# TensorE in source order for the whole kernel, and modulation matmuls released in other groups

## The chip, the cores and the metric

The kernel runs on one core of one Trainium2 chip. The metric is the device time of one execution in microseconds (us). TensorE multiplies matrices, VectorE and ScalarE do elementwise work, SyncE issues the DMA transfers. In the rows below PE is TensorE's matmuls, PEld its weight loads, DVE VectorE, ACT ScalarE, and SPq SyncE's queue.

## The reference, cut to what matters

Two layers run on 384 tokens: 128 context tokens and 256 denoising tokens, with 2048 channels in 16 blocks of 128. For one layer:

```
shift, scale, gate = split(silu(c) @ w_mod + b_mod)            # per channel, for two condition vectors
h = rmsnorm(x) * (1 + scale) + shift
f_x,f_g, p_x,p_g, q,k,v,a_g, c_a,c_b,c_g = split(h @ w_in)     # 11 chunks of 512
y = concat(fourier(f_x) w_f * silu(f_g),  pool(p_x) w_p * silu(p_g),
           rmsnorm(diff_attention(q,k,v)) * silu(a_g),  conv_module(c_a,c_b) * silu(c_g)) @ w_out
x = x + gate * y
```

After the second layer the result is normalized and written token by token. The arithmetic is in 32 bits. A large product is made of three matmuls: each operand is split into a rounded part (hi) and a rest (lo), and hi·hi, hi·lo and lo·hi are summed in one PSUM bank.

## The kernel before, in words

**Main matmuls.** The input chunks are computed one after the other by `in_chunk` (L447): eight weight tiles of two 128-blocks each, loaded into a raw buffer (`rawp`, five of them), split by ScalarE (`hi`, L219) and VectorE (`lo`, L220) into buffers that hold three tiles (`hip` and `lop`, six halves each), and used by 24 matmuls (`main_tile`, L439, `mm3`, L434) into four PSUM banks (`mm`). The output projection (L920 to L942) does the same in four groups of 512 channels, g = 0 to 3. In the last group one 128-block is completed after the other. `finish_block` (L901) adds a finished block to x, and in the second layer scales it by final_g on ScalarE and transposes it on TensorE into `otp` (L918), in the order of the source right behind the group's last main matmul.

**Tasks.** Smaller branches are Python generators in a list `tasks`: `attention` (L585), `fourier`, `small_proj`, `pool_proj`, `conv_norm`. After every tile of 24 main matmuls `pump` (L347) is called. It calls `step` (L376), which advances each task to its next `yield`. A task's step takes a small PSUM tile with `sm` (L103; three buffers) for its matmuls. The number of yields between two parts of a task is the number of main tiles that the source puts between them. `finish` (L371) advances a task to its end at once, with no main tile between its parts. It is called in `gate` (L858): the chunk A_G is computed, then `finish(at)` ends the attention, then the gate is multiplied, and the next chunk, F_G, follows. At that point of the source the attention still has to normalize its last head, transpose it (`asT`), multiply it by the values (`aso`), normalize the heads (`otok`) and transpose twelve blocks (`oT`).

**Modulation.** shift, scale and gate of what is still to come are computed by two queues of items in `pump`: `fill["pe"]`, items of one 512 KB load (`mraw`) and small 32-column matmuls into `mod` (`mod_item`, L253, matmuls at L277), and `fill["dve"]`, items computed on VectorE (`side_item`, sums on TensorE as `mds`). At each pump `rate` is added to `due`; the `pe` queue is released when two items are due (`BP`). In layer 0 there are 48 such items at 48/78 per pump, in layer 1 twelve at 12/45. Four more are issued at the layers' border (`pe_mods`).

**Who sets the order.** The kernel is written for a planner that takes the instructions in source order as priorities and orders each engine's queue by estimated times: an instruction whose operands it expects late is passed by later ones. `manual_schedule(engines=...)` takes the named engines out of the planning and keeps them in source order. Before, it holds SyncE and TensorE until `in_order.close()` (L825), that is, through the first four chunks of layer 0; after that the planner orders both. ScalarE and VectorE are planned throughout. Weight loads and their splitting run at a raised priority (`ahead`, L206) after L825.

Of the kernel before, what the change touches and what calls it, by code (L numbers as in the profile page):

```python
# [55 lines left out]
def mixer_step(  # L56
# [11 lines left out]
    NB1, NB2 = 2, 2  # L68
    YA = 5
    BP = 2  # L70
    WARM = 24

    one = ctx.enter_context(tc.tile_pool(name="one", bufs=1))
# [19 lines left out]
    def nm(s):  # L93
        uid[0] += 1
        return f"{s}_{uid[0]}"
# [4 lines left out]
    def cvtile(s):  # L100
        return cvp.tile([P, 4, 432], F32, tag="cv", name=nm(s))

    def sm(s, shape=(P, 512)):  # L103
        return smp.tile(list(shape), F32, tag="sm", name=nm(s))

    def tt(out, a, b, op, eng=None):
# [32 lines left out]


    in_order = ExitStack()
    in_order.enter_context(tc.manual_schedule(engines={mybir.EngineType.SP, mybir.EngineType.PE}))

    o1 = CONST_OFF["ident"][0] + P
    nc.sync.dma_start(out=cst[:, :o1], in_=consts[:, :o1])
# [13 lines left out]
    xd = [drp.tile([P, 4, NT], F32, tag=f"xd{g}", name=f"xd{g}") for g in range(4)]  # L159

    idle = sm("idle")
    for _ in range(WARM):
        nc.tensor.matmul(idle, lhsT=ones, rhs=cmod.rearrange("p k c -> p (k c)"), start=True, stop=True)  # L163
# [149 lines left out]
    def side_item(l, kind, b0, k0):  # L313
        pool = side_pool[0]
        key = (l, kind, b0)
        if k0 == 0:
            side_acc[key] = gtile(pool, "macc", (P, 2, 512))
        acc = side_acc[key]
        raw = gtile(pool, "sraw", (P, 2, 512))
        c0 = MOD.index(kind) * D + b0 * P  # L320
        with ahead():
            nc.sync.dma_start(out=raw, in_=w_src("w_mod", l, k0, c0))
        for j in range(2):
            for v in range(2):
                cv = cmod[:, k0 + j, v:v + 1]
                if k0 + j == 0:
                    nc.vector.tensor_scalar(out=acc[:, v, :], in0=raw[:, j, :], scalar1=cv, scalar2=None, op0=ALU.mult)
                else:
                    stt(acc[:, v, :], raw[:, j, :], cv, acc[:, v, :], ALU.mult, ALU.add)
        if k0 + 2 == KC:  # L330
            del side_acc[key]
            ps = sm("mds", (P, 2, 4, 32))
            av = acc.rearrange("p v (b n) -> p v b n", n=P)
            for v in range(2):
                for q in range(4):
                    qs = slice(32 * q, 32 * q + 32)
                    nc.tensor.matmul(ps[qs, v], lhsT=ones[:, 0:32], rhs=av[:, v, :, qs])
            T = one.tile([P, 2, 4, 32], F32, tag="S", name=nm("T"))
            nc.vector.transpose(out=T.rearrange("p v b n -> p (v b n)"), in_=ps.rearrange("p v b n -> p (v b n)"))
            mod_store(l, kind, b0, 4, T[:, :, :, 0].rearrange("p v b -> p b v"))  # L340

    fill = {"pe": [], "dve": []}
    rate = {"pe": 0.0, "dve": 0.0}
    due = {"pe": 0.0, "dve": 0.0}
    burst = {"pe": BP, "dve": 1}

    def pump(flush=False):  # L347
        step()
        for e, item in (("pe", mod_item), ("dve", side_item)):
            due[e] += rate[e]  # L350
            if fill[e] and (due[e] >= burst[e] or flush):
                n = len(fill[e]) if flush else int(due[e])
                for _ in range(min(n, len(fill[e]))):
                    due[e] -= 1.0
                    item(*fill[e].pop(0))
            if not fill[e]:
                due[e] = 0.0
# [7 lines left out]
    def advance(gen):  # L365
        try:
            next(gen)
        except StopIteration:
            tasks.remove(gen)
# [4 lines left out]
                advance(gen)  # L374

    def step():  # L376
        for gen in list(tasks):
            advance(gen)

    def share(l, units, n_side):  # L380
        n_pe = len(units) - n_side
        for i in range(n_pe):
            kind, b0 = units[i]
            if i % 2 == 0 and i + 1 < n_pe and units[i + 1] == (kind, b0 + 4):
                fill["pe"].extend(mod_wide(l, kind, b0))
            elif not (i % 2 and units[i - 1] == (kind, b0 - 4)):
                fill["pe"].extend(mod_items(l, ((kind, b0, 4),), 2))
        for kind, b0 in units[n_pe:]:
            fill["dve"].extend(side_items(l, kind, b0))
# [18 lines left out]
    def bcast_tokens(r):  # L408
        dg = tmpp.tile([P, TB, P], F32, tag="t1", name=nm("dg"))
        for t in range(TB):  # L410
            nc.vector.tensor_scalar(out=dg[:, t, :], in0=ident, scalar1=r[:, t:t + 1], scalar2=None, op0=ALU.mult)
        bc = sm("bc")
        nc.tensor.matmul(bc[:, :NT], lhsT=ones, rhs=dg.rearrange("p t k -> p (t k)"))
        return bc
# [32 lines left out]
    def in_chunk(l, ci, hh, hl):  # L447
        ps4 = [mmp.tile([P, 512], F32, tag="mm", name=nm("mm")) for _ in range(4)]
        for kt in range(8):
            hi, lo = wtile(w_src("w_in", l, 2 * kt, ci * BR))  # L450
            main_tile(ps4, hi, lo, (2 * kt, 2 * kt + 1), hh, hl, kt == 0, kt == 7)
            pump()
        return ps4

    def v_chunk(l, hh, hl):
        ps3 = [mmp.tile([P, 512], F32, tag="mm", name=nm("mm")) for _ in range(TB)]
        for kt in range(8):
            hi, lo = wtile(w_src("w_in", l, 2 * kt, V_ * BR))
            for j in range(2):
                kc = 2 * kt + j  # L460
                g, kb = divmod(kc, 4)
                for t in range(TB):
                    ts = slice(t * P, (t + 1) * P)
                    st = kt == 0 and j == 0
                    sp = kt == 7 and j == 1
                    nc.tensor.matmul(ps3[t], lhsT=hh[g][:, kb, ts], rhs=hi(j), start=st, stop=False)  # L466
                    nc.tensor.matmul(ps3[t], lhsT=hh[g][:, kb, ts], rhs=lo(j), start=False, stop=False)  # L467
                    nc.tensor.matmul(ps3[t], lhsT=hl[g][:, kb, ts], rhs=hi(j), start=False, stop=sp)  # L468
            pump()
        return ps3  # L470
# [308 lines left out]
    for l in range(DEPTH):  # L779
# [141 lines left out]
        for g in range(4):  # L921
            ps4 = [mmp.tile([P, 512], F32, tag="mm", name=nm("mm")) for _ in range(4)]
            if g < 3:
                for i, kt in enumerate(order):
                    hi, lo = wtile(w_src("w_out", l, 2 * kt, g * BR))
                    main_tile(ps4, hi, lo, (2 * kt, 2 * kt + 1), yh, yl, i == 0, i == 7)
                    pump()
# [34 lines left out]
    n = 0  # L962
# [130 lines left out]
```

## Time and profile before

| What | Value |
|---|---|
| median of three runs | 1260.34 us (1260.25 to 1261.93) |
| the profiled execution | 1259.32 us, span 1257.5 us |
| mean granted TensorE clock | 0.993 |
| busy share: PE, PEld, DVE, ACT | 98%, 91%, 73%, 44% |
| chain that ended last | PE 86%, DVE 7%, DMA 3% |

The span runs from the first to the last instruction. A matmul's duration in the trace overlaps with that of the next one, so the pitch (start to start) is what a matmul costs when many follow each other. A plain 32-bit matmul has two records (the 24 of the warm-up are 48), a main matmul or a transpose has one.

### The profile page before, as it was taken

What the parts mean: (1) busy time and instruction counts of PE and PEld (TensorE: products, weight loads), DVE (VectorE), ACT (ScalarE), POOL (GpSimd) and SP (SyncE); (2) the same over time, 40 slices, a digit from 0 to 9 for tenths busy, and PEclk for the clock granted to TensorE, in tenths of its full rate; (3) what the DMA queues carried; (4) which work ended last, traced back from release to release, by engine and by line L of the source; (5) the groups of instructions that cost most, each with busy time, mean ns of one, the idle gap of its engine ahead of it and who ended that gap; (6) DMA issues with size and microseconds to landing.
All of it is one profiled execution on the core that took longest, in us unless ns stands there. A gap on an engine that the chain in (4) does not pass through costs nothing.

```text
span 1257.5 us, 22096 instructions
## 1 busy us (share of the span) xinstructions
PE 1229.7 (98%) x8558; PEld 1145.4 (91%) x8558; DVE 921.6 (73%) x1788; ACT 555.8 (44%) x1116; POOL 2.1 (0%) x34
## 2 busy tenths in 40 slices
PE   8899999999999999999999999999999999999995
PEld 4899998798998999999998999979999999999995
DVE  3588788999965965998977559998455795647452
ACT  4533233344547545432235533334554765344442
POOL 0000000000000000000000000000000000000000
PEclk9899999999999999999999999999999999999998
DMA  6898887543446865888955444444223563645322
GB/s 239 294 354 313 299 307 274 176 170 116 149 157 206 287 232 188 312 307 306 333 204 184 160 151 159 159 160 149 94 88 115 176 243 118 201 156 187 118 67 101
DMA packets 70712, 251.85 MB, mean 200 GB/s; under 512 B 7760, under 2 KB 8912, under 8 KB 70608
## 3 DMA queue, kind: packets, MB, share of 16 engines
q1 hardware_dynamic: 70608, 250.45, 56.6%
q8 instruction: 67, 1.10, 0.3%
q14 instruction: 37, 0.30, 0.1%
HBM read 243.08 MB, written 7.34 MB: 199 GB/s over the span
## 4 chain that ended last, share of the span: by engine, by line
PE 86%; DVE 7%; DMA 3%; issue 2%; ACT 1%; SPq 0%; DVEq 0%; ACTq 0%
PE mm L435 23%; PE mm L437 22%; PE mm L436 22%; PE mod L277 4%; DVE cacc L110 2%; DVE lo L107 2%; PE idle L163 2%; PE mm L466 2%; PE mm L467 2%; PE mm L468 2%; DMA mraw<-in_w_mod_dram 1%; DMA sraw<-in_w_mod_dram 1%; PE sp L435 1%; PE sp L436 1%; PE sp L437 1%
## 5 line engine op out<-in xcount | busy, mean ns | idle before, releaser
L116 ACT ACTIVATE hi<-raw 128x512 fp32r<-128x512 f32 x498 | 309.1, 631 | 537.1 <-PE mm L436 349.0
L107 DVE TENSOR_TENSOR lo<-raw,hi 128x512 fp32r<-128x512 f32 x498 | 336.4, 687 | 213.5 <-ACT hi L116 204.6
L435 PE MATMUL mm<-hh,hi 128*128 128x384 f32 x1280 | 440.3, 345 | 5.3 <-ACT hh L113 5.2
L436 PE MATMUL mm<-hl,hi 128*128 128x384 f32 x1280 | 432.4, 338 | 0.0
L437 PE MATMUL mm<-hh,lo 128*128 128x384 f32 x1280 | 432.1, 338 | 0.0
L435 PEld LDWEIGHTS mm<-hh,hi 128*128 128x128 f32 x1280 | 241.5, 189 | 24.0 <-issue 9.9
L436 PEld LDWEIGHTS mm<-hl,hi 128*128 128x128 f32 x1280 | 241.8, 189 | 0.9 <-DVE hl L110 0.2
L437 PEld LDWEIGHTS mm<-hh,lo 128*128 128x128 f32 x1280 | 241.6, 189 | 0.3 <-DVE lo L107 0.3
L435 PE MATMUL mm<-yh,hi 128*128 128x384 f32 x512 | 173.5, 340 | 1.7 <-DVE xr L110 1.7
L436 PE MATMUL mm<-yl,hi 128*128 128x384 f32 x512 | 172.4, 337 | 0.0
L437 PE MATMUL mm<-yh,lo 128*128 128x384 f32 x512 | 172.4, 337 | 0.0
L110 DVE SCALAR_TENSOR_TENSOR macc<-sraw,cmod,macc 128x512 f32<-128x512 f32 x210 | 147.3, 743 | 8.1 <-DMA sraw<-in_w_mod_dram 8.1
L110 DVE SCALAR_TENSOR_TENSOR cacc<-u,cst,cacc 128x399 f32<-128x399 f32 x232 | 146.5, 631 | 6.0 <-ACT cacc L113 1.6
L435 PEld LDWEIGHTS mm<-yh,hi 128*128 128x128 f32 x512 | 96.2, 188 | 5.5 <-issue 3.6
L436 PEld LDWEIGHTS mm<-yl,hi 128*128 128x128 f32 x512 | 96.3, 188 | 0.0
L437 PEld LDWEIGHTS mm<-yh,lo 128*128 128x128 f32 x512 | 96.2, 188 | 0.0
L107 DVE TENSOR_TENSOR acc<-acc,mm 128x384 f32<-128x384 f32 x128 | 65.8, 551 | 25.9 <-PE mm L437 25.8
L277 PE MATMUL mod<-mraw,cmod 128*32 128x128 f32 (+2 forms) x1920 | 73.9, 290 | 1.4 <-DMA mraw<-in_w_mod_dram 0.9
L277 PEld LDWEIGHTS mod<-mraw,cmod 128*32 128x32 f32 x1920 | 48.0, 109 | 21.7 <-issue 11.5
L113 ACT ACTIVATE hh<-ht,AB 128x128 fp32r<-128x128 f32 x64 | 27.3, 451 | 26.4 <-DVE ht L110 25.6
L466 PE MATMUL mm<-hi,hh 128*128 128x512 f32 x96 | 38.3, 399 | 0.0
L467 PE MATMUL mm<-lo,hh 128*128 128x512 f32 x96 | 38.0, 396 | 0.0
(209 smaller groups left out, 956.7 us busy)
## 6 DMA issues: line engine op xcount, KB each, us to landing
raw<-in_w_in_dram SPq DMA_DIRECT2D x172, 512.0 KB, 4.4
mraw<-in_w_mod_dram SPq DMA_DIRECT2D x136, 512.0 KB, 4.6
raw<-in_w_out_dram SPq DMA_DIRECT2D x64, 512.0 KB, 4.3
sraw<-in_w_mod_dram SPq DMA_DIRECT2D x56, 512.0 KB, 5.7
xT<-in_x_dram SPq DMA_DIRECT2D x4, 768.0 KB, 6.7
xr<-in_x_dram SPq DMA_DIRECT2D x4, 768.0 KB, 7.0
xd<-xr SPq DMA_DIRECT2D x4, 768.0 KB, 5.8
xr<-xd SPq DMA_DIRECT2D x4, 768.0 KB, 5.9
```

The costliest lines, as they stand in the source:

```text
L107: (eng or nc.vector).tensor_tensor(out=out, in0=a, in1=b, op=op)
L110: nc.vector.scalar_tensor_tensor(out=out, in0=a, scalar=s, in1=b, op0=op0, op1=op1)
L113: nc.scalar.activation(out=out, in_=a, func=func, **kw)
L116: nc.scalar.activation(out=out, in_=a, func=AF.Copy, scale=scale)
L163: nc.tensor.matmul(idle, lhsT=ones, rhs=cmod.rearrange("p k c -> p (k c)"), start=True, stop=True)
L277: nc.tensor.matmul(ps[qs, 0:nb * 32].rearrange("p (b n) -> p b n", n=32), lhsT=cmod[:, k0 + j, :], rhs=raw[:, j, :, qs], start=(k0 + j == ...
L435: nc.tensor.matmul(ps, lhsT=wh, rhs=ah, start=start, stop=False)
L436: nc.tensor.matmul(ps, lhsT=wh, rhs=al, start=False, stop=False)
L437: nc.tensor.matmul(ps, lhsT=wl, rhs=ah, start=False, stop=stop)
L466: nc.tensor.matmul(ps3[t], lhsT=hh[g][:, kb, ts], rhs=hi(j), start=st, stop=False)
L467: nc.tensor.matmul(ps3[t], lhsT=hh[g][:, kb, ts], rhs=lo(j), start=False, stop=False)
L468: nc.tensor.matmul(ps3[t], lhsT=hl[g][:, kb, ts], rhs=hi(j), start=False, stop=sp)
```

## The change

TensorE's source order is entered on the kernel's own context, so it lasts to the end; SyncE's ends where it did. `pump` learns from `step` whether a task took a small PSUM tile in this step (`visits`), and releases the items of the `pe` queue when two are due and there was such a visit, or when four are due (`LATE`). Nothing that is computed changes.

```diff
+    LATE = 4
...
+    visits = []
+
     def sm(s, shape=(P, 512)):
+        visits.append(s)
         return smp.tile(list(shape), F32, tag="sm", name=nm(s))
...
     in_order = ExitStack()
-    in_order.enter_context(tc.manual_schedule(engines={mybir.EngineType.SP, mybir.EngineType.PE}))
+    ctx.enter_context(tc.manual_schedule(engines={mybir.EngineType.PE}))
+    in_order.enter_context(tc.manual_schedule(engines={mybir.EngineType.SP}))
...
     def pump(flush=False):
-        step()
+        visit = step()
         for e, item in (("pe", mod_item), ("dve", side_item)):
             due[e] += rate[e]
-            if fill[e] and (due[e] >= burst[e] or flush):
+            ready = due[e] >= (burst[e] if visit or e == "dve" else LATE)
+            if fill[e] and (ready or flush):
                 n = len(fill[e]) if flush else int(due[e])
...
     def step():
+        n = len(visits)
         for gen in list(tasks):
             advance(gen)
+        return len(visits) > n
```

## Rows read from the trace of the kernel before

**Rows 1.** The page's first part: busy us, share, instructions.

```profile
PE 1229.7 (98%) x8558; PEld 1145.4 (91%) x8558; DVE 921.6 (73%) x1788; ACT 555.8 (44%) x1116; POOL 2.1 (0%) x34
```

**Rows 2.** Window of tile mm alone in layer 1: us, PE, PEld, DVE, ACT, clock, DMA.

```profile
715.00:740.00 25.00, 25.00 (x146) 25.00 (x145) 0.00 (x0) 0.00 (x0) 1.00 0.38 128
```

**Rows 3.** Timeline of PE, first phase: start, us, instruction, idle before it.

```profile
64.85 0.64 PE L277 MATMUL mod<-mraw,cmod 128*32 128x128 f32 x16 [0.61 <-DMA mraw<-in_w_mod_dram]
```

**Rows 4.** Timeline of PE around a run of two modulation items.

```profile
255.91 0.34 PE L437 MATMUL mm<-hh,lo 128*128 128x384 f32 x1
256.18 1.07 PE L277 MATMUL mod<-mraw,cmod 128*32 128x256 f32 x16
257.18 0.45 PE L435 MATMUL mm<-hh,hi 128*128 128x384 f32 x1
257.46 0.34 PE L436 MATMUL mm<-hl,hi 128*128 128x384 f32 x1
```

**Rows 5.** Timeline of PE around a run of four items.

```profile
94.98 1.96 PE L277 MATMUL mod<-mraw,cmod 128*32 128x128 f32 x64
96.86 0.44 PE L435 MATMUL mm<-hh,hi 128*128 128x384 f32 x1
```

**Rows 6.** Timeline of PE, two items behind an attention step.

```profile
351.83 1.07 PE L277 MATMUL mod<-mraw,cmod 128*32 128x256 f32 x16
352.83 0.44 PE L435 MATMUL mm<-hh,hi 128*128 128x384 f32 x1
```

**Rows 7.** DMA issues, the page's sixth part: count, KB each, us to landing.

```profile
mraw<-in_w_mod_dram SPq DMA_DIRECT2D x136, 512.0 KB, 4.6
```

**Rows 8.** Timeline of PE at the end of layer 0's attention.

```profile
384.37 0.60 PE L640 MATMUL scs<-acc,acc 64*128 64x256 f32 x4
...
392.07 0.52 PE L657 MATMUL asT<-cst,pt 128*128 128x128 f32 x3
...
403.07 0.51 PE L680 MATMUL oT<-cst,otok 128*128 128x128 f32 x3
```

**Rows 9.** Windows of tile mm alone, where the planner moved TensorE's work.

```profile
384.97:403.30 18.33, 15.76 (x75) 12.98 (x75) 0.00 (x0) 1.25 (x3) 1.00 0.77 261
976.95:995.35 18.40, 16.41 (x81) 14.03 (x82) 0.00 (x0) 1.24 (x3) 1.00 0.54 184
1136.13:1141.80 5.67, 5.26 (x25) 4.07 (x25) 2.08 (x6) 0.00 (x0) 1.00 0.56 187
```

**Rows 10.** Timeline of ACT beside the first of these windows.

```profile
388.97 0.62 ACT L116 ACTIVATE hi<-raw 128x512 fp32r<-128x512 f32 x1
...
399.54 0.64 ACT L116 ACTIVATE hi<-raw 128x512 fp32r<-128x512 f32 x1
```

**Rows 11.** Timeline of PE in layer 1's output projection, behind group 0.

```profile
1138.23 0.49 PE L918 MATMUL otp<-cst,xr 128*128 128x128 f32 x3
...
1141.51 0.55 PE L918 MATMUL otp<-cst,xr 128*128 128x128 f32 x3
```

**Rows 12.** Timeline of DVE, then of PE, behind group 3's first block.

```profile
1216.60 0.74 DVE L110 SCALAR_TENSOR_TENSOR xr<-mm,GT,xr 128x128 f32<-128x128 f32 x2 [0.84 <-PE mm L437]
...
1218.65 0.50 PE L918 MATMUL otp<-cst,xr 128*128 128x128 f32 x3
```

**Rows 13.** Windows of all instructions (POOL before the clock), and a timeline row of PE.

```profile
36.00:43.00 7.00, 6.45 (x20) 6.21 (x21) 2.22 (x4) 3.93 (x9) 0.00 (x0) 0.51 0.63 253
670.00:675.00 5.00, 3.19 (x37) 1.62 (x36) 3.61 (x14) 2.78 (x7) 0.00 (x0) 1.00 0.91 311
...
36.55 0.69 PE L435 MATMUL mm<-hh,hi 128*128 128x384 f32 x1 [3.27 <-ACT hh L113]
```

**Rows 14.** Timeline of PE at the layers' border.

```profile
669.66 0.83 PE L418 MATMUL st<-ones,xsq 128*128 128x1 f32 x6
...
672.27 0.91 PE L413 MATMUL bc<-dg,ones 128*128 128x384 f32 x2
```

**Rows 15.** Timeline of PE inside a Fourier step of layer 0.

```profile
292.05 1.05 PE L277 MATMUL mod<-mraw,cmod 128*32 128x256 f32 x10
```

## The prediction

> **What bounds the kernel now.** I read the page's busy shares first: TensorE is busy for 1229.7 us of a span of 1257.5, VectorE for 921.6, ScalarE for 555.8 [rows 1]. So what TensorE doesn't do, or does at half clock, is added to the time. Next I took TensorE's timeline and cut it into islands: stretches of anything but main matmuls between two main matmuls. A main matmul alone has a pitch of 25.00 us over some 144.3 (146 touch the window, two are cut by its edges), 0.173 us [rows 2]. Then I laid the timeline beside the source. Nearly every island stands where the source has it. The reader is to see the exceptions [rows 8, 9, 11]: there the planner let main matmuls of the next chunk pass an instruction whose operands were late. The timelines of ScalarE and VectorE show why they were late [rows 10, 12].
>
> **Part 1: other groups of modulation matmuls.** In a run of two items the first record is 0.27 us behind the last main matmul, the run takes 1.00, and the next main pitch is 0.28 instead of 0.173 [rows 4]. A run of four takes 96.86 - 94.98 = 1.88 [rows 5]. So an item is (1.88 - 1.00) / 2 = 0.44, and a run by itself has a fixed cost of 0.12 in it, 0.10 on entering and 0.11 on leaving: 0.32. Two items behind an attention step take 352.83 - 351.83 = 1.00 again [rows 6], and there entering and leaving, 0.20, are paid by that step.
> By the source, the 48 items of layer 0 at 0.615 per pump are now 24 runs of two, 16 of them alone, and layer 1's twelve are six runs, five alone. With the visits and LATE I count 15 runs in layer 0 (7 alone) and 4 in layer 1 (2 alone). Eleven runs fewer at 0.12, and twelve fewer alone at 0.20: 1.3 + 2.4 = 3.7 us gained. Bounds: nothing (the cost goes with the item), and 5. The loads come in fours on SyncE's queue, 512 KB and 4.6 us each [rows 7], and hold four of the five raw buffers. Two converted weight tiles, 2 x 24 x 0.173 = 8.3 us of matmuls, and the fifth buffer cover that, so I add nothing; without that cover one run would wait about one landing, 4.6 us.
>
> **Part 2: source order to the end.** It costs wherever TensorE's next instruction has late operands. SyncE's and GpSimd's queues aren't reordered by the edit after the first phase. What stands behind a late instruction on TensorE is the next chunk's main matmuls, and on those wait the evacuations, the freeing of hi and lo, and so the weight loads. That source order does block is seen in the first phase, where TensorE waits 0.61 us for a modulation load with main matmuls behind it [rows 3].
>
> *End of the attention, once per layer.* Behind the last tile of A_G, `finish(at)` issues asT, aso and oT with nothing between them. In layer 0 they end 18.33 us after the last scores [rows 8, 9]: maxima on VectorE, exponentials, normalizing, asT, a copy, aso, squares, a root, twelve scalings, oT. Before, 75 main matmuls of chunk F_G, 75 x 0.173 = 13.0 us, ran in that stretch, and 81 in layer 1's 18.40 us, 14.0 us [rows 9]. In source order they come after. The chain gets shorter, since the splitting of F_G's weights, which stood in ScalarE's queue between its parts, can't run while the buffers are full: four copies (the first and the last are shown [rows 10]) of 0.63, some 2.5 us. So 18.33 becomes about 15.9. Loss: 15.9 + 13.0 - 18.33 = 10.6 in layer 0, 15.9 + 14.0 - 18.40 = 11.5 in layer 1; the run of two items in layer 0's window (0.9) comes later as well: 23.0 in all. Bounds for both: 17 (chain of 13) and 28 (chain as before).
>
> *Clock behind that wait.* TensorE now stands still from the scores to asT, 392.07 - 384.97 = 7.1 us before, some 6 with the shorter chain. After an idle of 3.27 us the trace shows the granted clock at 0.51, the lower level, for 36 to 43, where 20 main matmuls took 6.45 us instead of 3.5 [rows 13]: 3.0 us lost. After a shorter idle, in the window 670 to 675 with 3.19 of 5.00 us busy, the clock stayed at 1.00 [rows 13]. I take 3.0 for each of the two ends, 6.0; bounds 0 and 9 (the small matmuls slow as well). The Trainium skill, "TensorE: Matmul & The Clock Gate", section "HAM oscillation — how this bites in real kernels", speaks against the change here: gaps of TensorE between bursts bring the clock down. The row at 0.51 agrees; without any such fall the sum would be 6.0 lower.
>
> *Output projection of layer 1, groups 0 to 2.* The four otp steps stand behind the group in the source. Behind group 0 (end 1136.13) the planner placed them at 1138.23 to 1141.51 [rows 11] and ran 25 main matmuls, 4.3 us, between them [rows 9]. In source order TensorE waits for VectorE's sum and ScalarE's scaling of each block. One splitting copy less (0.63) makes 5.67 into 5.0. Loss: 5.0 + 4.3 - 5.67 = 3.6; groups 1 and 2 have the same pattern, three times: 10.9. Bounds: 6 (only the wait for the first block) and 16 (nothing overlaps).
>
> *Group 3, blocks 0 to 2.* Each block's otp now stops the next block: from the block's end, just ahead of VectorE's sum at 1216.60, say 1216.45, to 1218.65 [rows 12], 2.2 us, three times: 6.6. Bounds 5 and 8. Block 3 waits before and after.
>
> *Two small places.* At the layers' border mds and modulation filled the wait for the last sums (669.66) and for bc (672.27) [rows 14]; in source order they follow the sums and push bc back by about 0.9. In the Fourier step a modulation run of 1.0 us filled a wait for small PSUM buffers [rows 15], and four main matmuls did in layer 1: 1.8. Bounds for the three: 0 and 5.
>
> **Sum.** -3.7 + 23.0 + 6.0 + 10.9 + 6.6 + 0.9 + 1.8 = 45.5 us over the profiled execution's own 1259.32: 1304.8. The median of before lies 1.0 above that execution, so 1305.8.
>
> **Rivals.**
> *A. The waits are shorter.* The planner now knows that TensorE waits, and ScalarE and VectorE may serve the chains first. With the lower bounds, 17 + 0 + 6 + 5 - 3.7 = 24: 1285. For: table loads and copies stand in the chain. Against: the steps depend on each other, none can be left out.
> *B. The clock falls at the group borders too.* The three stretches of 5 us would hold twelve small transposes each and nothing else. That is less than in the window 670 to 675 that kept its clock, but the longest single gap, some 2 us, is under the 3.27 of the row that lost it [rows 11, 13]. At 3.0 each, 9 more: 1315. The Trainium skill, "TensorE: Matmul & The Clock Gate", section "Part 4: PE-mode transpose", says that transposes don't count as TensorE activity for the clock, which would favour this; no row separates it, since main matmuls stood between these transposes.
> *C. Faster: the waits don't come and the grouping remains.* If TensorE's later queue stayed planned, or if the attention ended within A_G's tiles, only Part 1 would be left: 1260.3 - 3.7 = 1256.6. The place is the chain from the last scores to oT; it decides once all waits together are below 3.7 us, a twelfth of what I sum. For: the edit would then only thin out the switching, which the rows price. Against: `finish` puts no main matmul between those parts, and the first phase shows source order blocking [rows 3].
> *D. No change,* waits just as large as the gain: 1260.
>
> **How the numbers follow.** Forecast 0.56 (its own range 1292 to 1316), A 0.13, B 0.20, C 0.08, D 0.03. A, B and the forecast are slower: 0.89. Faster by over 0.2% only in C, 0.08; within 0.2%, about what a measurement of this kernel can tell from no change, 0.03. The predicted time is the forecast's, 1306. The range is 1280 to 1322: it holds most of A's and B's spread beside the forecast's own bounds, and leaves out C, D and the outer ends, together under 0.2.
>
> **What the changed kernel's profile would show.** Between the last scores and oT of each layer no main matmul, and waits of asT, aso and oT of 5 to 10 us in total per layer; a granted clock near 0.5 for some us at the start of F_G; 2 us of waiting ahead of the first otp of groups 0 to 2 and ahead of each of group 3's; 19 modulation runs in place of 30. The prediction is wrong if main matmuls still stand between asT and oT, if TensorE's waits add up to less than 15 us, or if they appear at places not named here, such as mds sums waiting for VectorE or modulation waiting for its loads.

## The result, and the profile after

The changed kernel takes 1348.49 us (median of four runs, 1344.62 to 1352.56) against 1260.3: a ratio of 1.0708, 95% interval 1.0687 to 1.0728, 88.2 us slower. The direction was forecast; the size was 45.5, and the time lies outside the range of 1280 to 1322. The profiled execution took 1349.12, with a span of 1347.3.

First the busy shares, as in [rows 1]: the work is the same, TensorE's share of the span has fallen from 98% to 93%.

```profile
PE 1258.8 (93%) x8558; PEld 1172.1 (87%) x8558; DVE 926.4 (69%) x1788; ACT 556.2 (41%) x1116; POOL 2.1 (0%) x34
```

The span is 89.8 us longer. TensorE's idle time in it grew from 1257.5 - 1229.7 = 27.8 us to 1347.3 - 1258.8 = 88.5, so 60.7 us are waits; in the other 29.1 the same 8558 instructions are busy for longer, which is where a lower clock shows.

TensorE's waits, most in total first (us in total, times, longest): first the top of the view before, then the view after. Line numbers are those of each kernel's own source.

```profile
PE mm L435 <- ACT hh L113: 5.2, 2, 3.3
PE idle L163 <- ACT cmod L113: 4.0, 1, 4.0
PE mm L435 <- DVE xr L110: 1.7, 3, 1.1
```

```profile
PE otp L926 <- ACT xr L120: 15.5, 12, 2.0
PE asT L665 <- DVE pt L114: 12.5, 2, 6.2
PE mm L443 <- ACT sg L117: 7.6, 4, 3.4
PE oT L688 <- ACT otok L120: 6.6, 2, 3.3
...
PE mod L282 <- DVE T L287: 5.5, 4, 2.9
...
PE mm L443 <- DVE xr L114: 3.8, 4, 1.6
PE mm L474 <- ACT q L781: 3.4, 1, 3.4
```

otp, asT and oT are places that I had named. The waits of main matmuls for `sg` (Silu of a gate's chunk), `xr` (the sum into x) and `q`, and of modulation for `T` (its transposed result) are not: there another engine is still reading the PSUM bank that TensorE is to write next.

TensorE's timeline at the end of layer 0's attention (start, us, instruction, idle before it), which answers to [rows 8]:

```profile
386.04 0.60 PE L648 MATMUL scs<-acc,acc 64*128 64x256 f32 x4
392.87 1.54 PE L665 MATMUL asT<-cst,pt 128*128 128x128 f32 x6 [6.23 <-DVE pt L114]
...
400.56 2.82 PE L688 MATMUL oT<-cst,otok 128*128 128x128 f32 x9 [3.29 <-ACT otok L120]
404.24 0.90 PE L688 MATMUL oT<-cst,otok 128*128 128x128 f32 x3 [0.87 <-ACT mixa L120]
404.79 0.67 PE L443 MATMUL mm<-hh,hi 128*128 128x384 f32 x1
```

No main matmul stands between the scores and oT, as forecast, and the chain, from the end of the scores to the next main matmul, took 404.79 - 386.64 = 18.2 us, not 15.9. Part of the small matmuls in it ran at half clock, that is, at a granted clock near 0.5. Behind group 0 and behind group 3's first two blocks [rows 11, 12]:

```profile
1203.03 1.05 PE L926 MATMUL otp<-cst,xr 128*128 128x128 f32 x6 [1.88 <-ACT xr L120]
1204.75 0.55 PE L926 MATMUL otp<-cst,xr 128*128 128x128 f32 x3 [0.67 <-ACT xr L120]
1205.82 0.59 PE L926 MATMUL otp<-cst,xr 128*128 128x128 f32 x3 [0.52 <-ACT xr L120]
...
1300.13 0.55 PE L926 MATMUL otp<-cst,xr 128*128 128x128 f32 x3 [2.04 <-ACT xr L120]
...
1311.05 0.55 PE L926 MATMUL otp<-cst,xr 128*128 128x128 f32 x3 [2.04 <-ACT xr L120]
```

Windows of the changed kernel (us, then PE, PEld, DVE, ACT, POOL busy, granted clock, DMA), as in [rows 13]: the end of the attention, C_G's first tile in layer 0, and in the output projection behind group 0, behind group 2, and behind the first and the second block of group 3.

```profile
385.00:400.00 15.00, 6.04 (x31) 4.74 (x29) 6.06 (x15) 10.04 (x22) 0.00 (x0) 0.77 0.41 123
404.00:412.00 8.00, 7.76 (x38) 7.76 (x39) 7.06 (x14) 4.62 (x10) 0.00 (x0) 0.78 0.18 66
...
497.00:503.00 6.00, 5.95 (x19) 5.96 (x20) 4.71 (x10) 3.40 (x8) 0.31 (x3) 0.50 0.11 44
1206.40:1209.50 3.10, 3.10 (x12) 3.10 (x11) 0.00 (x0) 1.34 (x3) 0.00 (x0) 0.50 1.02 412
1288.20:1291.60 3.40, 3.40 (x12) 3.40 (x12) 0.00 (x0) 1.16 (x3) 0.00 (x0) 0.51 0.02 5
1300.40:1309.00 8.60, 8.60 (x51) 8.29 (x49) 2.08 (x3) 2.03 (x4) 0.00 (x0) 1.00 0.00 0
1312.00:1315.20 3.20, 3.20 (x12) 3.20 (x11) 0.00 (x0) 0.48 (x1) 0.00 (x0) 0.50 0.00 0
```

C_G's first tile waits ahead of its first matmul. TensorE's row, and ScalarE's beside it: the Silu (`sg`) that reads P_G's banks comes behind the last part of the conv norm (`csh`).

```profile
497.05 0.69 PE L443 MATMUL mm<-hh,hi 128*128 128x384 f32 x1 [3.35 <-ACT sg L117]
...
495.70 0.92 ACT L120 ACTIVATE csh<-u 128x384 fp32r<-128x384 f32 x2
496.52 1.60 ACT L117 ACTIVATE sg<-mm 128x384 f32<-128x384 f32 x4
```

Counting main matmuls of 384 columns with a pitch near 0.32 in the timelines gives 115 in the changed kernel and 16 before: 99 more at 0.147 each, 14.5 us, of which I had only foreseen those behind oT (7 in layer 0, 11 in layer 1).

The modulation runs. A run of four alone [rows 5], and one that crosses from one accumulation group into the next:

```profile
268.98 1.94 PE L282 MATMUL mod<-mraw,cmod 128*32 128x256 f32 x32
270.85 0.44 PE L443 MATMUL mm<-hh,hi 128*128 128x384 f32 x1
...
543.58 1.08 PE L282 MATMUL mod<-mraw,cmod 128*32 128x128 f32 x32
547.58 1.93 PE L282 MATMUL mod<-mraw,cmod 128*32 128x128 f32 x32 [2.92 <-DVE T L287]
549.45 0.69 PE L443 MATMUL mm<-yh,hi 128*128 128x384 f32 x1
```

The run alone costs 1.87 as priced, and there are 19 runs, as counted. The other run takes 5.87: there is one PSUM bank for modulation (`mdp`), and the next group's first matmul waits until VectorE has transposed the last group out of it.

### The profile page after: what moved, and what is told of

It reads as the page before. It is cut to its first block, busy times and chain, and to the rows that moved or that the text cites. A ratio compares the mean times of both kernels' runs of the same rounds, so it can differ in the third digit from the quotient of the medians.

```text
span 1347.3 us, 22088 instructions
## 1 busy us (share of the span) xinstructions
PE 1258.8 (93%) x8558; PEld 1172.1 (87%) x8558; DVE 926.4 (69%) x1788; ACT 556.2 (41%) x1116; POOL 2.1 (0%) x34
## 4 chain that ended last, share of the span: by engine, by line
PE 67%; DVE 8%; ACT 5%; DMA 2%; issue 2%; DVEq 0%; ACTq 0%
PE mm L443 19%; PE mm L444 18%; PE mm L445 18%; DVE lo L111 2%; PE mod L282 2%; DVE macc L114 1%; DVE cacc L114 1%; ACT hi L120 1%; DMA raw<-in_w_in_dram 1%; PE mm L474 1%; PE mm L475 1%; PE mm L476 1%; PE sp L445 1%; PE sp L444 1%; PE aso L672 1%
## 5 line engine op out<-in xcount | busy, mean ns | idle before, releaser
L443 PEld LDWEIGHTS mm<-hh,hi 128*128 128x128 f32 x1280 | 244.9, 191 | 33.0 <-issue 10.4
L444 PEld LDWEIGHTS mm<-hl,hi 128*128 128x128 f32 x1280 | 244.8, 191 | 1.4 <-DVE hl L114 0.8
L445 PEld LDWEIGHTS mm<-hh,lo 128*128 128x128 f32 x1280 | 244.7, 191 | 1.0 <-DVE lo L111 1.0
L443 PE MATMUL mm<-yh,hi 128*128 128x384 f32 x512 | 178.4, 349 | 3.8 <-DVE xr L114 3.8
L444 PE MATMUL mm<-yl,hi 128*128 128x384 f32 x512 | 175.7, 343 | 0.0
L444 PEld LDWEIGHTS mm<-yl,hi 128*128 128x128 f32 x512 | 99.4, 194 | 0.0
L476 PE MATMUL mm<-hi,hl 128*128 128x512 f32 x96 | 38.5, 401 | 0.0
```

What stands on the lines that cost most here:

```text
L443: nc.tensor.matmul(ps, lhsT=wh, rhs=ah, start=start, stop=False)
L444: nc.tensor.matmul(ps, lhsT=wh, rhs=al, start=False, stop=False)
L445: nc.tensor.matmul(ps, lhsT=wl, rhs=ah, start=False, stop=stop)
```

## The experiments

Each ratio is to the kernel before, run on the same chip beside it (medians 1258.9 to 1259.8), with its 95% interval. Differences between two kernels are differences of medians; the ratios give them with some 4 to 6 us of room on either side.

**1. Source order alone.** Runs by twos as before:

```diff
-    LATE = 4
+    LATE = 2
```

> The changed kernel with LATE = 2: TensorE in source order, items released by twos as before. Theory 1 (source order costs all of it, the grouping gains what its switching rows say): 3.7 us slower than the changed kernel, about 1352. Theory 2 (in source order the bursts cost too: runs of three and four cross the end of an accumulation group, waits on T 5.1 us with half clock behind two of them, and hold the raw buffers so that weight tiles come late, 3.4 at V of layer 1 and some 5 in layer 0's output projection): 10 to 16 us faster than the changed kernel, 1333 to 1339, with T waits under 1 us.

1332.27 us, ratio 1.0559 (1.0520 to 1.0598), 16 us faster than the changed kernel: the new grouping costs, as theory 2 has it. Among TensorE's waits, T is back at the level of before, and none for q is listed.

```profile
PE mod L282 <- DVE T L287: 0.4, 1, 0.4
```

**2. Grouping alone.** `visits` and `LATE = 4`, TensorE held in source order in the first phase only:

```diff
-    ctx.enter_context(tc.manual_schedule(engines={mybir.EngineType.PE}))
-    in_order.enter_context(tc.manual_schedule(engines={mybir.EngineType.SP}))
+    in_order.enter_context(tc.manual_schedule(engines={mybir.EngineType.SP, mybir.EngineType.PE}))
```

> The kernel before with visits and LATE = 4, TensorE's order planned after the first phase. Theory 1: the switching saved shows, 1260.3 - 3.7 = 1256.6. Theory 2: the planner moves main matmuls into the waits that bursts make, so the gain shows as well or is half eaten: 1256 to 1260, and not slower than before.

1270.13 us, ratio 1.0079 (1.0053 to 1.0105): slower than before by some 0.8%, against both theories' numbers. The planner splits crossing runs and puts main matmuls between, but not enough of them: a row of its timeline still shows 2.50 us.

```profile
526.73 1.08 PE L281 MATMUL mod<-mraw,cmod 128*32 128x128 f32 x32 [2.50 <-DVE T L286]
```

**3. The attention ends inside A_G's tiles.** The changed kernel with fewer yields, and one more ahead of oT:

```diff
-    YC1, YC2, YC3, YT = 1, 4, 1, 2
+    YC1, YC2, YC3, YT = 1, 4, 1, 1
-    YA = 5
+    YA = 2
...
-        yield
+        for _ in range(2):
+            yield
         sg = tiny.tile([P, 1], F32, tag="sg", name=nm("sg"))
```

> The changed kernel with the attention's yields cut (YA 2 in place of 5, YT 1 in place of 2, two yields in place of one ahead of oT), so that it ends within A_G's tiles and finish finds nothing left. If the two ends of the attention cost what I summed (23.0 of chain and 6.0 of clock): 25 to 30 us faster than the changed kernel, 1319 to 1324, no wait of asT above 1 us. If the waits only move to earlier attention steps, which now stand closer together: less than 10 us faster.

1313.8 us, ratio 1.0426 (1.0396 to 1.0457): 34.7 us faster than the changed kernel. Waits of asT and oT, 20.8 us in all, are gone from the list, so the two ends did cost about what I had summed, 29.0, or more. How much more isn't shown: in this profile the waits for q (1.8 us) and hh (4.9), which lie elsewhere, are 2.8 us shorter too, and the wait for q varies between 1.6 and 3.9 us over the profiles of the kernels that release in fours.

**4. The transposes one tile later.** `finish_block` puts (g, b) into a list, and one block is transposed after each following tile of main matmuls:

```diff
-                for t in range(TB):
-                    nc.tensor.transpose(outs[t][:, b * P:(b + 1) * P], x[:, t * P:(t + 1) * P], ident)
+                late.append((g, b))
...
                     pump()
+                    late_block()
```

> The changed kernel with the second layer's transposes of finished blocks put one main tile later in the source, so that TensorE has 4 us of main matmuls ahead of each. Waits of otp are 15.5 us in the changed kernel, and the clock stands at half behind four of the group or block ends, 38 main matmuls at 0.32 in place of 0.173 or 5.6 us. If both go: 18 to 22 us faster, 1327 to 1331. If only the waits go and the clock falls from something else: 14 to 16 us faster.

1323.87 us, ratio 1.0510 (1.0478 to 1.0541): 24.6 us faster. otp waits for nothing any more; the waits of main matmuls for VectorE's sum, which frees their bank, grew from 3.8 us to 7.0:

```profile
PE mm L443 <- DVE xr L114: 7.0, 5, 2.5
```

**5. No run crosses a group.** The changed kernel, a run ends with its accumulation group:

```diff
-                    item(*fill[e].pop(0))
+                    it = fill[e].pop(0)
+                    item(*it)
+                    if e == "pe" and not flush and it[2] + it[3] == KC:
+                        break
```

> The changed kernel, but a run of modulation items ends with the last item of its accumulation group, so no run crosses into the next group. The changed kernel waits 5.5 us for T, 5.1 of it more than before, with half clock behind the longest (543 us). If the crossings make most of the 16 us that releasing by twos gave back: 1336 to 1340. If the loads in fours make it (raw buffers held, weight tiles late): 1341 to 1344, T waits below 1 us, waits for q at V and for xr in the output projection still there.

1337.68 us, ratio 1.0620 (1.0583 to 1.0657), faster than the changed kernel's 1.0687 to 1.0728: by the medians 11 of the 16 us, by the ratios something between 6 and 16. T waits 0.4 us in all, 5.1 less than in the changed kernel. What is left against releasing by twos (1.0520 to 1.0598) is inside the intervals' overlap; the wait for q is still there:

```profile
PE mm L477 <- ACT q L784: 3.9, 1, 3.9
```

In the changed kernel ScalarE's timeline shows what stands ahead of it. The copy of q out of PSUM comes behind weight splits (`hi`) that wait for their load:

```profile
851.97 1.15 ACT L120 ACTIVATE hi<-raw 128x512 fp32r<-128x512 f32 x2 [4.44 <-DMA raw<-in_w_in_dram]
853.30 0.63 ACT L120 ACTIVATE hi<-raw 128x512 fp32r<-128x512 f32 x1 [0.18 <-DMA raw<-in_w_in_dram]
853.83 1.22 ACT L781 COPY q<-mm 128x384 f32<-128x384 f32 x3
```

In total ScalarE's `hi` waits 119 us for weight loads before, 112 in source order by twos (1), 173 in the changed kernel and 197 here. So with items in fours the loads land later even with five raw buffers; what part of that reaches TensorE these sums don't tell.

**6. The conv norm one tile earlier.** Source order by twos, with YC2 = 3:

```diff
-    YC1, YC2, YC3, YT = 1, 4, 1, 2
+    YC1, YC2, YC3, YT = 1, 3, 1, 2
```

> Source order, items by twos (as the run that gave 1332.3), with the conv norm's YC2 = 3 in place of 4, so that its last part is issued one main tile earlier and ScalarE reaches the Silu of P_G before C_G's first tile needs its PSUM bank. If that wait (3.35 us in each layer, and 10 main matmuls at 0.32 behind it, 1.5 us) is the order of ScalarE's queue: 9 to 10 us faster, 1322 to 1324. If the wait just moves to the conv norm's sums (mean, st, bc): no gain, 1330 to 1333.

1322.35 us, ratio 1.0504 (1.0483 to 1.0525): by the medians 9.9 us faster than source order by twos, as expected; the intervals just touch (1.0520 to 1.0598 there). The waits for `sg` fall from 7.2 us, which is the wait that the edit was to take away:

```profile
PE mm L443 <- ACT sg L117: 1.1, 3, 0.5
```

**7. All four together in source order** (the edits of 1, 3, 4 and 6).

> Source order with all four at once: items by twos, attention inside A_G, transposes one tile later, YC2 = 3. If the causes add up: 1332.3 - 34.7 - 24.6 - 9.7 = 1263, level with the kernel before within a few us. If the waits were sharing one cause (a late engine that shows up elsewhere once a wait is taken away): above 1280.

1281.36 us, ratio 1.0174 (1.0151 to 1.0196). Most comes back, 67 of the 88 us, but the single gains don't add up: 18 us more than their sum. Of TensorE's waits, those for VectorE's sum and in the Fourier steps (fa) are longer than in the changed kernel, the one of apT is new, and the kernel stays slower than before:

```profile
PE mm L443 <- DVE xr L114: 9.5, 6, 2.5
...
PE fa L696 <- ACT pt L117: 2.2, 2, 1.3
PE fa L696 <- ACT u L703: 2.0, 3, 0.7
PE apT L626 <- DVE pp L114: 1.7, 3, 1.2
```

**8. Matmuls that only keep TensorE running.** The changed kernel; their result isn't used:

```diff
+    def fillers(n):
+        spare = sm("spare")
+        for _ in range(n):
+            nc.tensor.matmul(spare, lhsT=ones, rhs=cmod.rearrange("p k c -> p (k c)"), start=True, stop=True)
...
+            if h == 3:
+                fillers(6)
             for _ in range(YT):
...
+        fillers(3)
         r = rstd_cols(ss, 12, 1.0 / P)
```

> The changed kernel with matmuls added that nothing uses: six of 512 columns ahead of asT and three ahead of oT of the last head, in both layers, about 1 us each, in waits of 6.2 and 3.3 us. Behind these waits 7 and 11 main matmuls ran at half clock (2.6 us) and asT, aso and oT between them too (asT and aso took 1.3 us more than at other heads). If the clock falls because TensorE stands still, it stays at 1.00 there and the time falls by 3 to 6 us, to 1343 to 1346; if the clock falls for another reason, no gain, or up to 3 us slower where the added matmuls run over the wait.

1344.89 us, ratio 1.0673 (1.0633 to 1.0713): the median is 3.6 lower, the intervals overlap, so the total isn't told apart. The clock is. In layer 0 the two stretches that read 0.77 and 0.78 in the changed kernel now read 1.00, with main matmuls from 400.95 on; the first row below ends the scores:

```profile
384.11 0.60 PE L653 MATMUL scs<-acc,acc 64*128 64x256 f32 x4
400.95 0.42 PE L443 MATMUL mm<-hh,hi 128*128 128x384 f32 x1
...
385.00:400.00 15.00, 12.98 (x45) 6.16 (x43) 7.86 (x18) 11.62 (x31) 0.00 (x0) 1.00 0.61 199
404.00:412.00 8.00, 8.00 (x48) 8.00 (x48) 7.84 (x13) 2.63 (x5) 0.00 (x0) 1.00 0.38 131
1034.60:1037.00 2.40, 2.40 (x10) 2.40 (x9) 2.32 (x6) 2.04 (x5) 0.00 (x0) 0.54 0.61 218
```

The chain from the last scores to the first main matmul took 400.95 - 384.71 = 16.2 us instead of 18.2. Nothing but the filled waits differs there, so in layer 0 the fall came from TensorE standing still. In layer 1 the chain kept 1.00 as well up to oT, but the last transposes and the first main matmuls behind them ran at half clock again (the third window), behind waits of 0.72 and 1.02 us. Elsewhere this execution lost the clock where the changed kernel's had not: from 449 to 453 us it read 0.59, behind a wait for `sg` of 1.60 us that was 0.67 in the changed kernel. So the total says little of what the clock costs.

**9. The three moves under the planner** (the edits of 3, 4 and 6, items by twos, TensorE planned).

> TensorE's order planned as in the kernel before, items by twos, with the three moves that helped source order (attention inside A_G, transposes one tile later, YC2 = 3). The planner already filled those waits with main matmuls, so the moves can only save switching: some twenty single transposes that stand between main matmuls now, 0.1 us each: 1256 to 1260. If they disturb the planner's other orders: up to 1275.

1265.42 us, ratio 1.0036 (1.0021 to 1.0051): a little slower than before, outside 1256 to 1260 and inside the second range, that the moves disturb the planner's other orders. What helps source order gains nothing where the planner already filled the waits; what costs the 5 us stays open.

**10. Grouping alone, no crossing, under the planner** (the edits of 2 and 5).

> TensorE's order planned, the new grouping, but a run ends with its accumulation group. The grouping alone gave a ratio of 1.0079, some 10 us slower than before, with waits on T of 3.6 us. If the crossings are the cause: 1257 to 1262, the switching gain shows. If the raw buffers held by fours are the cause (ScalarE's waits for weight loads were 162 us with the grouping, 119 before): 1264 to 1270.

1266.1 us, ratio 1.0041 (1.0022 to 1.0060) against 1.0079 (1.0053 to 1.0105) with crossings. The point values put some 4 of the 10 us on the crossings, but the intervals overlap at their ends, so that isn't shown. The time lies in the range that I had given to the raw buffers, and no gain of the switching shows.

**11 and 12. Four raw buffers in place of five**, with runs of up to four (the kernel of 5), and by twos (the kernel of 1):

```diff
-    rawp = ctx.enter_context(tc.tile_pool(name="rawp", bufs=5))
+    rawp = ctx.enter_context(tc.tile_pool(name="rawp", bufs=4))
```

> The changed kernel with runs that end with their group (1337.7 with five raw buffers), and four raw buffers in place of five, so that a run of four holds all of them. If bursts cost through the raw buffers: at least 8 us slower than with five, 1346 or more, and more than the same cut costs when items go by twos. If the fifth buffer is spare in both: within 3 us of 1338.

> Source order, items by twos (1332.3 with five raw buffers), with four raw buffers. The control for the run beside it: if raw buffers matter through the bursts, this cut costs less than half of what it costs there, 0 to 5 us: 1332 to 1337. If buffers bound the loads everywhere: as much as there.

1383.3 us, ratio 1.0978 (1.0950 to 1.1006), and 1338.43 us, 1.0614 (1.0592 to 1.0636): the same cut costs 45.6 us with fours and 6.2 with twos, just over the 0 to 5 that I had expected. With fours, main matmuls now wait for their weights, with twos 0.5 us:

```profile
PE mm L446 <- ACT hi L120: 32.4, 9, 5.5
```

So with four raw buffers a run of four holds up the main stream's weights. No version tried beats the kernel before.

## Why the prediction was wrong, point by point

**The view that I read, and its reach.** Islands in the wrong place named the waits that the planner had filled with much work. I didn't ask of every main matmul whether its PSUM bank would be free: at C_G's first tile the old trace showed `small_proj`'s matmuls ahead of the tile that stands before them in the source, and I took that for nothing. One row of `small_proj` there, from the kernel before:

```profile
474.62 0.80 PE L435 MATMUL sp<-csh,hi 128*128 128x384 f32 x3
```

By the signs that I had named the prediction was wrong: waits stood at `sg`, `xr`, `q` and `T`, places not in it.

**End of the attention: right, too small.** Summed 23.0 and 6.0, measured 34.7 by experiment 3. The chain took 18.2 us, and 16.2 at full clock (experiment 8), near my 15.9; most of the difference is asT and aso, from the start of the first to the end of the last 4.4 us at half clock and 2.7 at full.

**Output projection: right, too small.** Summed 17.5, measured 24.6 by experiment 4. otp's waits, 15.5, agree; what I left out of the forecast was the clock, 38 main matmuls at 0.147, 5.6 us. It fell behind groups 0 to 2 and behind one of group 3's blocks: rival B's mechanism, where the longest single waits were 1.5 to 2.0 us.

**Part 1: the step that failed, with the wrong sign.** "3.7 us gained", and "the fifth buffer cover that, so I add nothing". Measured: 16 us lost in source order (1), 10 planned (2). The price of switching was right, a run of four takes 1.87. Not seen: accumulation groups hold 8 or 16 items, and runs of two end with them, while the new runs, of two to four, cross at the 24th, 32nd and 40th item. That is by the medians 11 of the 16 us in source order. The rest would fit the raw buffers, which 11 and 12 show to bind with fours when there are only four of them; how much of it they make with five isn't settled, and no run with more than five was made.

**The other step that failed: C_G's first tile, put at nothing.** P_G's banks are freed by Silu on ScalarE, which stands behind the conv norm's last part. It cost 3.35 us of waiting per layer and the half clock behind it, together 9.9 us by the medians of 1 and 6.

**Small places.** The Fourier wait and the layers' border came where forecast, the border larger: 707.20 - 702.36 = 4.8 us from sums to bc instead of 2.6 [rows 14], where I had 0.9 more. Part of that is the clock again, 0.56 in these 3.30 us, where the kernel before had 1.00:

```profile
702.36 0.83 PE L426 MATMUL st<-ones,xsq 128*128 128x1 f32 x6 [1.51 <-ACT xsq L117]
707.20 1.21 PE L421 MATMUL bc<-dg,ones 128*128 128x384 f32 x2
...
704.00:707.30 3.30, 3.30 (x41) 1.48 (x33) 2.38 (x8) 1.15 (x2) 0.00 (x0) 0.56 1.03 364
```

These single measurements, 34.7 + 24.6 + 16.2 + 9.9 = 85.4, come close to the 88.2. That is partly luck and no proof that the account is complete: all together give back 67 (experiment 7). My reading, argued and not shown, is that when one wait is taken away TensorE reaches the next late operand sooner, so that a single gain includes slack that others need too. Which of the 18 us belongs to which wait stays open.

## What to carry to other kernels

Before putting an engine's queue in source order, go through the source and ask of every instruction what its operands and its output bank need from other engines since the last work that could hide it; a step that runs to its end at once shows its whole chain. A gap of TensorE can cost more than its own length: behind many of those here the main matmuls ran at half clock. A grouping that saves switching is to be checked against what it holds: accumulation groups with one bank, and load buffers that the main stream shares.

## What the runs showed of the hardware that I had not expected

The clock fell behind shorter waits as well, not only behind 3.27 us [rows 13], and not every time. In group 3 a single wait of 2.04 us stood three times ahead of three transposes. Behind the ones at 1300.13 and 1323.52 the granted clock stayed at 1.00; behind the one at 1311.05 it read 0.50 from 1312.00 on, a few main matmuls later. Behind groups 0, 1 and 2 it fell each time, to 0.50, 0.52 and 0.51, but there TensorE ran no main matmul for 5.0 to 5.8 us, and between its waits mostly small transposes, so these cases don't tell what a gap of a certain length does. What decided between the cases no run here shows.

The Trainium skill, "TensorE: Matmul & The Clock Gate", section "HAM oscillation — how this bites in real kernels", ties the fall to gaps between bursts; experiment 8 agrees in layer 0, 0.77 becoming 1.00 with the gap filled. The Trainium skill, "TensorE: Matmul & The Clock Gate", section "Part 4: PE-mode transpose", says that a transpose doesn't count as busy in the same way; no run here separates the transposes from the short waits around them.
